# First norm's squares taken from the transposed input on chip, and the residual stream loaded later

## The chip, the cores and the metric

The kernel runs on one NeuronCore of a Trainium2 chip. Its engines run side by side, each through its own list of instructions in order: TensorE (PE: matmuls, with PEld for the loads of their stationary operand), VectorE (DVE), ScalarE (ACT), GpSimd (POOL) and SyncE (SP), which issues most of the DMAs. They wait for one another through semaphores. The metric is the device time of one execution in microseconds (us), the median of several runs; lower is better.

## The reference

One layer of a decoder in float32, on 256 tokens of width 1024: a gated feed-forward network (FFN) at half weight, a mixing layer with two branches, a second FFN at half weight, and a last norm. Cut to what matters here:

```python
def rmsnorm(x, g):
    y = xf * lax.rsqrt(jnp.mean(xf * xf, axis=-1, keepdims=True) + EPS)
    return y * g
def swiglu(x, w_gate, w_up, w_down):
    return (jax.nn.silu(x @ w_gate) * (x @ w_up)) @ w_down
h = x
h = h + 0.5 * swiglu(rmsnorm(h, ffn1_norm), ffn1_w_gate, ffn1_w_up, ffn1_w_down)
n = rmsnorm(h, mix_norm)
...
h = h + merged @ w_out
h = h + 0.5 * swiglu(rmsnorm(h, ffn2_norm), ffn2_w_gate, ffn2_w_up, ffn2_w_down)
return rmsnorm(h, final_norm)
```

The FFN's hidden width is 2816. The change concerns the first norm, `rmsnorm(h, ffn1_norm)` with h = x.

## The kernel before

**Precision and units.** The weights come from memory in units of 1 MB, each as two halves of 512 KB (`raw`, a ring of 7 buffers) on SP's queue. ACT casts each half to a high part and DVE subtracts to get a low part (`split`, L205 and L207); both go to `w`, a ring of 4 units. Each product is then three matmuls: high by high, high by low, low by high (`mm3`, L191 to L193). A unit's cast therefore waits until TensorE has left the unit four places earlier, and a load waits until DVE has left the half seven places earlier.

**The first FFN.** Its 11 chunks of 256 gate and 256 up columns take two units each: chunk c uses units 2c and 2c + 1, so chunk zero has units 0 and 1, chunk one units 2 and 3. TensorE runs 48 matmuls a chunk, 24 a unit. Unit 22 is the first of the down projection.

**The front.** The input and chunk zero's weights come together, transposed, in eight rows (`front`, 128 partitions; row k holds 256 columns of x for 128 features, then 512 of weights). ACT and DVE split each row as it lands (the loop over k), and TensorE follows with chunk zero (L491 to L495). x is only multiplied by the norm's gain there; the norm's factor per token, which is one over the root of the mean square, is applied to the chunk's result, in `glu` (L403, L405). Ahead of it TensorE runs 16 warm-up matmuls on zeros (L94).

**The norm's factor.** `square` (L231) squares the residual stream on ACT in four pieces of 128x512, `token_sums` (L237) adds the eight feature blocks on DVE in three steps, `sum_parts` splits the sum in a high and low part (`sqp`, ACT and DVE), and `token_factors` adds over partitions with one matmul by ones (`sums`, L247), takes each token's value by four reductions on DVE (L255) and raises it to the power -0.5 on POOL (L259).

**What is squared.** `h` is a second copy of x, loaded by two DMAs of 512 KB from the same array in memory (L480). It is also the residual stream to which the down projection adds its result (L318).

**The order.** TensorE and SP run in the order in which the code is written. ACT and DVE run in the written order too inside `in_order()` blocks; elsewhere a scheduler orders them. A call of `unit` makes splits up to a number of units ahead (`ALONE` 3, `PAIRED` 2), and those splits stand on ACT and DVE where the call stands. Before the change, `unit(f1, PAIRED)`, `unit(f1 + 1, PAIRED)` and `chunk(f1, nT, "f1", 1, [0])` put the splits of units 2 to 5 ahead of the squares. The matmul of the sums stands on TensorE behind chunk one.

**The hidden values' way.** After each chunk DVE transposes the gated product in 32x32 blocks (`f1t`), SP sends it to memory (`leave`, `f1way`), and brings it back in another order (`arrive`, `f1back`, one buffer) in six groups; `settle` splits a group to `f1h`, which the down projection uses. `move(c)` and `rest()` place these steps between the chunks and in the down projection. SP's queue carries them in order among the loads of the weights.

Of the kernel before, what the change touches and what calls it, by code (L numbers as in the profile page):

```python
# [20 lines left out]
S = 256  # L21
NT = S // P
DFF = 2816
KB = D // P
# [9 lines left out]
CH = 256  # L34
NC = DFF // CH
FIRST = 2
# [2 lines left out]

ALONE = RING - 1  # L40
PAIRED = RING - 2
WARM = 16


@with_exitstack
def block_kernel(ctx, tc, t, out):
    nc = tc.nc
# [10 lines left out]
    def bank(name):  # L58
        return psum.tile([P, 512], F32, tag="ps", name=name)
# [3 lines left out]
    h = act.tile([P, KB, S], F32, tag="h", name="h")  # L63
# [3 lines left out]
    ROW = S + 2 * CH  # L67
    front = act.tile([P, 2 * FB * S], F32, tag="aT", name="front")

    def load_front(queue, k, end, c0=0, c1=ROW):  # L70

        a, b = KB * (k + c0 > 0) + k * ROW + c0, KB + (end - 1) * ROW + c1
        queue.dma_start(front[:, a:b], t["first"][:, a:b])
# [18 lines left out]
    wps = bank("warm")  # L92
    for i in range(WARM):
        nc.tensor.matmul(wps[:, :S], zeros[:, :P], zeros, start=True, stop=True)  # L94
# [5 lines left out]
    def add_units(name, n):  # L100
        first = len(units)
        units.extend((name, i) for i in range(n))
        return first
# [3 lines left out]
    f1 = add_units("f1", 2 * NC)  # L107
# [16 lines left out]
    def unit_tile(i):  # L124
        a, b = t[units[i][0]].shape[2:]
        parts[i] = wp.tile([P, a, 2, b], F32R, tag="w", name=f"w{i}")

    def half(i, hf):
        a = t[units[i][0]].shape[2]
        return slice(hf * a // 2, (hf + 1) * a // 2)  # L130

    def fetch_to(n):

        while fetched[0] < min(n, 2 * len(units)):
            i, hf = divmod(fetched[0], 2)
            fetched[0] += 1
            name, u = units[i]
            _, p, a, b = t[name].shape
            raws[i, hf] = rawp.tile([P, a // 2, b], F32, tag="raw", name=f"raw{i}_{hf}")
            nc.sync.dma_start(raws[i, hf], t[name][u][:, half(i, hf), :])  # L140

    def split_half(later=False):

        i, hf = divmod(done_to[0], 2)
        if hf == 0:
            unit_tile(i)
        fetch_to(done_to[0] + RAW)
        done_to[0] += 1
        w, sl = parts[i], half(i, hf)
        return split(w[:, sl, 0, :], w[:, sl, 1, :], raws.pop((i, hf)), later)  # L150

    def split_to(n):
        while done_to[0] < 2 * min(n, len(units)):
            split_half()
        fetch_to(done_to[0] + RAW)

    def unit(i, ahead=PAIRED):
        split_to(i + 1 + ahead)
        return parts[i]
# [29 lines left out]
    def mm3(ps, st, mv_, first, last):  # L189
        (sh, sl), (mh, ml) = st, mv_  # L190
        nc.tensor.matmul(ps, sh, mh, start=first, stop=False)  # L191
        nc.tensor.matmul(ps, sh, ml, start=False, stop=False)  # L192
        nc.tensor.matmul(ps, sl, mh, start=False, stop=last)  # L193
# [10 lines left out]
    def split(hi, lo, src, later=False):  # L204
        nc.scalar.copy(hi, src)  # L205
        def rest():
            nc.vector.tensor_sub(lo, src, hi.bitcast(F32))  # L207
        return rest if later else rest()

    def alloc_T(name, tags):  # L210

        return [act.tile([P, 4, 2, S], F32R, tag=tag, name=f"{name}{c}") for c, tag in enumerate(tags)]
# [4 lines left out]
    def block_of(nT, k):  # L217
        return both_of(nT, k)[:, 0, :], both_of(nT, k)[:, 1, :]

    def in_order():  # L220

        return tc.manual_schedule(engines={mybir.EngineType.DVE, mybir.EngineType.Activation})
# [3 lines left out]
    def square(hh, pair, name, tag=None):  # L226

        if pair == 0:
            squares[name] = act.tile([P, KB, S], F32, tag=tag, name=f"sq{name}")
        two = slice(2 * pair, 2 * pair + 2)  # L230
        nc.scalar.activation(squares[name][:, two, :], hh[:, two, :], AF.Square, scale=D ** -0.5)  # L231

    def token_sums(name, engine=nc.vector):

        sq = squares[name]
        for n in (4, 2, 1):
            engine.tensor_add(sq[:, :n, :], sq[:, :n, :], sq[:, n:2 * n, :])  # L237

    def sum_parts(name):
        sq = squares[name]  # L240
        squares[name] = tmp.tile([P, 2, S], F32R, tag="hg", name=f"sqp{name}")
        split(squares[name][:, 0, :], squares[name][:, 1, :], sq[:, 0, :])
# [132 lines left out]
    def chunk(i0, nT, name, c, us=range(2), ps=None):  # L375


        if ps is None:
            ps = [bank(f"{name}_{c}{j}") for j in range(NT)]
        for u in us:  # L380
            w = unit(i0 + 2 * c + u, ALONE)
            for k in range(4):
                for j in range(NT):
                    st = tuple(p[:, j * P:(j + 1) * P] for p in block_of(nT, 4 * u + k))
                    mm3(ps[j], st, (w[:, k, 0, :], w[:, k, 1, :]), u + k == 0, u == 1 and k == 3)
        return ps
# [59 lines left out]


    nT = alloc_T("n1", ("nA", "nB"))
    for i in range(FIRST):
        unit_tile(i)  # L450
    for k in range(KB):
        if k > 1:
            load_front(nc.sync, k, k + 1)
        row = front[:, KB + k * ROW:KB + (k + 1) * ROW]
        x, w, g = row[:, :S], row[:, S:], front[:, k:k + 1]
        x_hi, x_lo = block_of(nT, k)
        hi, lo = (parts[k // 4][:, k % 4, q, :] for q in range(2))

        def x_high():
            nc.scalar.activation(x_hi, x, AF.Identity, scale=g)  # L460

        def x_low():
            nc.vector.scalar_tensor_tensor(x_lo, x, g, x_hi.bitcast(F32), op0=ALU.mult, op1=ALU.subtract)

        if k:
            x_high()
            x_low()
            split(hi, lo, w)
            continue

        with in_order():
            x_high()
            nc.vector.tensor_copy(hi[:, :CH], w[:, :CH])
            nc.scalar.copy(hi[:, CH:], w[:, CH:])
            x_low()
            for c in (slice(0, CH), slice(CH, 2 * CH)):
                nc.vector.tensor_sub(lo[:, c], w[:, c], hi[:, c].bitcast(F32))
    fetch_to(2 * FIRST + 4)
    for c in range(2):
        nc.sync.dma_start(h[:, 4 * c:4 * c + 4, :],  # L480
                          t["first"][:, KB:].rearrange("p (k c) -> p k c", k=KB)[:, 4 * c:4 * c + 4, :S])
    hidden = Hidden("f1")

    sums = [[bank(f"f1_0{j}") for j in range(NT)]]
    unit(f1, PAIRED)
    for k in range(KB):
        hi, lo = (parts[k // 4][:, k % 4, q, :] for q in range(2))
        st = [tuple(p[:, j * P:(j + 1) * P] for p in block_of(nT, k)) for j in range(NT)]
# [4 lines left out]
            nc.tensor.matmul(sums[0][j], st[j][1], hi, start=False, stop=False)  # L493
        for j in range(NT):
            nc.tensor.matmul(sums[0][j], st[j][0], lo, start=False, stop=k == KB - 1)  # L495
    unit(f1 + 1, PAIRED)

    with in_order():
        sums.append(chunk(f1, nT, "f1", 1, [0]))
        for pair in range(KB // 2):  # L500
            square(h, pair, "1", "nC")
        token_sums("1")
        sum_parts("1")
        chunk(f1, nT, "f1", 1, [1], sums[1])
        rs = token_factors("1")
        sums.append(chunk(f1, nT, "f1", 2))
        for c in range(2):
            hidden.glu(c, sums[c], rs)
    for c in range(2, NC):
        if c > 2:  # L510
            sums.append(chunk(f1, nT, "f1", c))
            for moved in (1, 2, 3) if c == 3 else (c,):
                hidden.move(moved)
        hidden.glu(c, sums[c], rs)
# [94 lines left out]
    for j in range(NT):  # L609
# [4 lines left out]
        for a0 in range(0, HEADS // 2, per):  # L614

            pair = [bank(f"sc{j}{a0}{two}") for two in range(2)]
# [104 lines left out]
    for f in range(KB):  # L721
        i = mb + 2 * (f // 4)
        ps = bank(f"pb{f}")
        c = slice(f % 4 * P, (f % 4 + 1) * P)
        for q, bT in enumerate((aoT, gmT)):
            w = unit(i + q)
# [12 lines left out]
    with in_order():  # L739
        down_features(mo, 4, lambda k: both_of(mT, k), 1.0, gain3, nT3, "3", "aT")  # L740
        hidden = Hidden("f2")
        sums = [chunk(f2, nT3, "f2", 0)]
# [139 lines left out]
```

## Time and profile before

| | |
|---|---|
| median of 3 runs | 536.08 us (535.26 to 536.53) |
| the profiled execution | 536.36 us |
| its span, first to last instruction | 534.6 us |
| mean granted clock of TensorE in it | 0.992 |
| TensorE (PE) busy | 522.3 us, 98% of the span |
| DVE busy | 367.6 us, 69% |
| ACT busy | 273.4 us, 51% |
| moved by DMA | 118.72 MB, 222 GB/s in the mean |

Times inside the execution are in us from the span's start. A row of the timeline has start, duration, engine, line, operation, output and input, and in brackets how long the engine stood idle before it and who released it; `x3` is three such instructions merged. A row with SPq is the issue of DMAs. A matmul of 512 columns is listed with 0.39 us, but they overlap: one starts every 0.23 us, so it is the distance of the starts that counts. A row of the waits has the waiting engine, tile and line, who was waited for, the us in total, the times and the longest. A row of the windows has the stretch and its length, then the busy time of PE, PEld, DVE, ACT and POOL with the count of instructions, then TensorE's granted clock (1.00 is full), the DMA engines' share and GB/s.

### The profile page before, as it was taken

The page shows a single profiled execution, that of the slowest core. Times are in us where ns is not written, and L with a number is a line of the kernel's source. Part 1 is how long each engine was busy: PE and PEld are TensorE (multiplying, and loading weights), DVE is VectorE, ACT ScalarE, POOL GpSimd, SP SyncE. Part 2 cuts the span into 40 slices and gives each one's busy share as a digit, 9 for nine tenths or more (in the row PEclk, how much of TensorE's full clock was granted, in tenths as well). Part 3 has the DMA queues.
Part 4 walks back from the last instruction along what each step waited for, and adds up shares of the span by engine and source line. Part 5 has one row for each costly group of instructions (what it writes and reads, how often), then busy time and mean ns, then how long its engine had stood idle before and what let it go on. Part 6 is the DMA issues. An engine that isn't in the chain of part 4 may idle for free.

```text
span 534.6 us, 7273 instructions
## 1 busy us (share of the span) xinstructions
PE 522.3 (98%) x2667; PEld 443.9 (83%) x2667; DVE 367.6 (69%) x568; ACT 273.4 (51%) x401; POOL 11.5 (2%) x20
## 2 busy tenths in 40 slices
PE   8969999999999999999999999999999999999995
PEld 6858888888888888888888999888888888888884
DVE  6676666575346498987999878689665665565424
ACT  7546355454335257546887645366453544463402
POOL 0010000000000001000000000001000000000002
PEclk9979999999999999999999999999999999999999
DMA  8976699869968507875469646339789779677302
GB/s 320 395 282 206 191 309 263 245 221 260 261 177 285 188 29 244 318 226 169 118 178 360 220 140 200 126 118 346 231 255 308 226 269 323 191 237 227 142 1 78
DMA packets 52420, 118.72 MB, mean 222 GB/s; under 512 B 6817, under 2 KB 26785, under 8 KB 52385
## 3 DMA queue, kind: packets, MB, share of 16 engines
q1 hardware_dynamic: 52096, 117.94, 68.0%
q8 instruction: 21, 0.34, 0.3%
q10 hardware_dynamic: 288, 0.33, 0.2%
q14 instruction: 15, 0.11, 0.1%
HBM read 108.81 MB, written 9.44 MB: 221 GB/s over the span
## 4 chain that ended last, share of the span: by engine, by line
PE 92%; DMA 4%; DVE 1%; ACT 1%; issue 0%; POOLq 0%; SPq 0%; DVEq 0%; POOL 0%; ACTq 0%
PE f L191 14%; PE f L192 14%; PE f L193 14%; PE acc L165 10%; PE pgate L165 6%; PE acc L170 5%; PE acch L191 4%; PE acch L192 4%; PE acch L193 4%; DMA raw<-in_f 3%; PE pgate L170 3%; PE pq L165 3%; PE pb L191 1%; PE pb L193 1%; PE pb L192 1%; PE pq L170 1%
## 5 line engine op out<-in xcount | busy, mean ns | idle before, releaser
L207 DVE TENSOR_TENSOR w<-raw,w 128x1024 fp32r<-128x1024 f32 x180 | 212.9, 1217 | 68.4 <-ACT w L205 67.8
L205 ACT CAST w<-raw 128x1024 fp32r<-128x1024 f32 x180 | 180.4, 1049 | 94.2 <-PE f L193 47.0
L191 PE MATMUL f<-w,n 128*128 128x512 f32 x336 | 131.7, 392 | 0.0
L192 PE MATMUL f<-w,n 128*128 128x512 f32 x336 | 131.5, 391 | 0.0
L193 PE MATMUL f<-w,n 128*128 128x512 f32 x336 | 131.4, 391 | 0.0
L193 PEld LDWEIGHTS f<-w,n 128*128 128x128 f32 x336 | 63.6, 189 | 13.4
L192 PEld LDWEIGHTS f<-w,n 128*128 128x128 f32 x336 | 63.6, 189 | 13.3
L191 PEld LDWEIGHTS f<-w,n 128*128 128x128 f32 x336 | 63.6, 189 | 13.2
L165 PE MATMUL acc<-f1h,w 128*128 128x512 f32 x176 | 43.4, 391 | 0.0
L165 PEld LDWEIGHTS acc<-f1h,w 128*128 128x128 f32 x176 | 31.9, 188 | 5.8
L191 PE MATMUL acch<-w,f2h 128*128 128x512 f32 x84 | 32.7, 389 | 0.0
L192 PE MATMUL acch<-w,f2h 128*128 128x512 f32 x84 | 32.7, 389 | 0.0
L193 PE MATMUL acch<-w,f2h 128*128 128x512 f32 x84 | 32.7, 389 | 0.0
L165 PE MATMUL pgate<-n,w 128*128 128x512 f32 x128 | 32.6, 394 | 0.0
L165 PEld LDWEIGHTS pgate<-n,w 128*128 128x128 f32 x128 | 23.0, 189 | 4.4 <-issue 0.2
L403 ACT ACTIVATE f2s<-f,rstd 128x256 f32<-128x256 f32 x22 | 10.3, 474 | 29.3 <-PE f L193 29.3
L170 PEld LDWEIGHTS acc<-f1h,w 128*128 128x128 f32 x176 | 23.5, 191 | 1.5
L405 DVE SCALAR_TENSOR_TENSOR f2a<-f,rstd,f2s 128x256 f32<-128x256 f32 x22 | 10.5, 476 | 20.7 <-ACT f2s L403 20.7
L170 PE MATMUL acc<-f1h,w 128*128 128x256 f32 x176 | 23.9, 282 | 0.0
L403 ACT ACTIVATE f1s<-f,rstd 128x256 f32<-128x256 f32 x22 | 10.2, 473 | 22.7 <-PE f L193 18.4
L318 DVE SCALAR_TENSOR_TENSOR h<-acc,h 128x256 f32<-128x256 f32 x32 | 13.6, 424 | 10.1 <-PE acc L165 8.1
L191 PEld LDWEIGHTS acch<-w,f2h 128*128 128x128 f32 x84 | 15.8, 188 | 3.3
(166 smaller groups left out, 635.9 us busy)
## 6 DMA issues: line engine op xcount, KB each, us to landing
raw<-in_f SPq DMA_DIRECT2D x84, 512.0 KB, 6.1
raw<-in_f1d SPq DMA_DIRECT2D x22, 512.0 KB, 5.9
raw<-in_f2d SPq DMA_DIRECT2D x22, 512.0 KB, 6.8
raw<-in_gate SPq DMA_DIRECT2D x16, 512.0 KB, 4.3
raw<-in_qk SPq DMA_DIRECT2D x8, 512.0 KB, 5.6
raw<-in_out SPq DMA_DIRECT2D x8, 512.0 KB, 4.6
f1way<-f1t SPq DMA_DIRECT2D x11, 256.0 KB, 6.3
f2way<-f2t SPq DMA_DIRECT2D x11, 256.0 KB, 6.0
```

The lines of the kernel that those rows point to most:

```text
L165: nc.tensor.matmul(ps, st, both.rearrange("p two n -> p (two n)"), start=first, stop=last)
L170: nc.tensor.matmul(ps[:, n:], st, both[:, 0, :], start=False, stop=False)
L191: nc.tensor.matmul(ps, sh, mh, start=first, stop=False)
L192: nc.tensor.matmul(ps, sh, ml, start=False, stop=False)
L193: nc.tensor.matmul(ps, sl, mh, start=False, stop=last)
L205: nc.scalar.copy(hi, src)
L207: nc.vector.tensor_sub(lo, src, hi.bitcast(F32))
L318: nc.vector.scalar_tensor_tensor(h[:, c, :], acc[c][:, q * S:(q + 1) * S], scale, h[:, c, :], op0=ALU.mult, op1=ALU.add)
L403: nc.scalar.activation(sg, ps[j][:, :CH], AF.Silu, scale=rs[j])
L405: nc.vector.scalar_tensor_tensor(a, ps[j][:, CH:], rs[j], sg, op0=ALU.mult, op1=ALU.mult)
```

## The change

Three things are edited. The squares read x in `front`, that is the copy that is already on the chip for the matmuls, and not `h`. They stand behind the splits of unit 2 (`split_to(f1 + 3)`; `f1` is 0), with the halves of unit 3 split one before and one after the additions; all of this is inside `in_order()`. `h` is loaded later, by the same two DMAs, behind chunk two's code and the first products. Beside that, `WARM` is 17 for 16, the loop over k splits its rows inside `in_order()` for every k, two more halves are fetched in one go, and the tile of the hidden values is allocated later, since it takes the memory of `front`.

```diff
-WARM = 16
+WARM = 17
...
     nT = alloc_T("n1", ("nA", "nB"))
+
+    def inputs_of(rows):
+        return rows.rearrange("p (k c) -> p k c", k=KB)[:, :, :S]
...
-        if k:
-            x_high()
-            x_low()
-            split(hi, lo, w)
-            continue
-
         with in_order():
             x_high()
-            nc.vector.tensor_copy(hi[:, :CH], w[:, :CH])
-            nc.scalar.copy(hi[:, CH:], w[:, CH:])
+            if k == 0:
+
+                nc.vector.tensor_copy(hi[:, :CH], w[:, :CH])
+                nc.scalar.copy(hi[:, CH:], w[:, CH:])
+            else:
+                nc.scalar.copy(hi, w)
             x_low()
-            for c in (slice(0, CH), slice(CH, 2 * CH)):
+            for c in (slice(0, CH), slice(CH, 2 * CH)) if k == 0 else (slice(0, 2 * CH),):
                 nc.vector.tensor_sub(lo[:, c], w[:, c], hi[:, c].bitcast(F32))
-    fetch_to(2 * FIRST + 4)
-    for c in range(2):
-        nc.sync.dma_start(h[:, 4 * c:4 * c + 4, :],
-                          t["first"][:, KB:].rearrange("p (k c) -> p k c", k=KB)[:, 4 * c:4 * c + 4, :S])
-    hidden = Hidden("f1")
+    fetch_to(2 * FIRST + 6)
 
     sums = [[bank(f"f1_0{j}") for j in range(NT)]]
-    unit(f1, PAIRED)
...
-    unit(f1 + 1, PAIRED)
 
     with in_order():
-        sums.append(chunk(f1, nT, "f1", 1, [0]))
+        x = inputs_of(front[:, KB:KB + KB * ROW])
+        split_to(f1 + 3)
         for pair in range(KB // 2):
-            square(h, pair, "1", "nC")
+            square(x, pair, "1", "nC")
+        split_half()
         token_sums("1")
+        split_half()
         sum_parts("1")
-        chunk(f1, nT, "f1", 1, [1], sums[1])
+        sums.append(chunk(f1, nT, "f1", 1))
         rs = token_factors("1")
         sums.append(chunk(f1, nT, "f1", 2))
+        hidden = Hidden("f1")
         for c in range(2):
             hidden.glu(c, sums[c], rs)
+    for c in range(2):
+        nc.sync.dma_start(h[:, 4 * c:4 * c + 4, :], inputs_of(t["first"][:, KB:])[:, 4 * c:4 * c + 4])
```

On ACT, at chunk one, the rows before the change are these; `w2` is unit 2, `raw2_0` its first half, `sq1` the squares and `sqp1` their split sum:

```order
L205 CAST w2_177<-raw2_0_164 128x2x512
L205 CAST w2_177<-raw2_1_166 128x2x512
L205 CAST w3_242<-raw3_0_168 128x2x512
L205 CAST w3_242<-raw3_1_170 128x2x512
L205 CAST w4_255<-raw4_0_178 128x2x512
L205 CAST w4_255<-raw4_1_180 128x2x512
L205 CAST w5_262<-raw5_0_182 128x2x512
L205 CAST w5_262<-raw5_1_186 128x2x512
L231 ACTIVATE sq1_297<-h_80 128x512 x4
L205 CAST sqp1_305<-sq1_297 128x256
```

and in the changed kernel, on ACT at the same place:

```order
L205 CAST w2_252<-raw2_0_186 128x2x512
L205 CAST w2_252<-raw2_1_188 128x2x512
L231 ACTIVATE sq1_263<-front_81 128x512 x4
L205 CAST w3_268<-raw3_0_190 128x2x512
L205 CAST w3_268<-raw3_1_192 128x2x512
L205 CAST sqp1_278<-sq1_263 128x256
L205 CAST w4_283<-raw4_0_194 128x2x512
```

The squares have moved ahead of unit 3, the cast of their sum ahead of unit 4, and they read `front`. On DVE, at the same place, the changed kernel has (before, the three additions and `sqp1` stood behind `w5`):

```order
L207 TENSOR_TENSOR w2_252<-raw2_1_188,w2_252 128x2x512
L207 TENSOR_TENSOR w3_268<-raw3_0_190,w3_268 128x2x512
L237 TENSOR_TENSOR sq1_263<-sq1_263 128x1024
L237 TENSOR_TENSOR sq1_263<-sq1_263 128x512
L237 TENSOR_TENSOR sq1_263<-sq1_263 128x256
L207 TENSOR_TENSOR w3_268<-raw3_1_192,w3_268 128x2x512
L207 TENSOR_TENSOR sqp1_278<-sq1_263,sqp1_278 128x256
L207 TENSOR_TENSOR w4_283<-raw4_0_194,w4_283 128x2x512
```

The additions now stand between the halves of unit 3. On SP the two loads of `h` have moved from ahead of `raw4_0` to between `raw12_0` and `raw12_1`. TensorE's rows are the same but for one more warm-up matmul.

The scheduler also puts some later rows of ACT and DVE in another order. On ACT, where the first FFN's chunks end, the rows before are (`f1s100` and `f1s101` belong to the last chunk's gated product, `f1back3` and `f1back4` to the fourth and fifth group of hidden values):

```order
L205 CAST w24_1086<-raw24_1_970 128x1024
L205 CAST f1h_174<-f1back3_1035 128x8x4x32
L403 ACTIVATE f1s100_1123<-f1_100_1051,rstd1_354 128x256
L403 ACTIVATE f1s101_1128<-f1_101_1052,rstd1_354 128x256
L205 CAST w25_1197<-raw25_0_974 128x1024
L205 CAST w25_1197<-raw25_1_1003 128x1024
L205 CAST f1h_174<-f1back4_1192 128x8x4x32
```

and in the changed kernel, on ACT at the same place:

```order
L205 CAST w24_1108<-raw24_1_992 128x1024
L403 ACTIVATE f1s100_1145<-f1_100_1073,rstd1_373 128x256
L403 ACTIVATE f1s101_1150<-f1_101_1074,rstd1_373 128x256
L205 CAST w25_1219<-raw25_0_996 128x1024
L205 CAST w25_1219<-raw25_1_1025 128x1024
L205 CAST f1h_443<-f1back3_1057 128x8x4x32
L205 CAST f1h_443<-f1back4_1214 128x8x4x32
```

The fourth group's cast has moved from ahead of the last products to behind unit 25; DVE's subtraction moves likewise.

## The prediction

> **What bounds the kernel now.** I read the page first, then who waits for whom on TensorE, and then the timeline around the one long wait.
>
> ```profile
> span 534.6 us, 7273 instructions
> PEclk9979999999999999999999999999999999999999
> PE 92%; DMA 4%; DVE 1%; ACT 1%; issue 0%; POOLq 0%; SPq 0%; DVEq 0%; POOL 0%; ACTq 0%
> PE sums L247 <- DVE sqp L207: 4.5, 1, 4.5
> PE warm L94 <- DVE zeros L91: 1.2, 1, 1.2
> ```
>
> The chain that ended last lies 92% on TensorE, and the list of waits has for its matmuls, over the whole span, only the two quoted and one of 0.4 at the start (its row stands further down). So TensorE is the bound nearly everywhere, and what keeps it still is worth its full length. The one wait of size is the single matmul at L247, which adds the first norm's squares. It costs more than the 4.5 us of its row, as the third slice of the clock row (7 tenths) hints. The next fence is TensorE's timeline: start, duration, instruction.
>
> ```profile
> 17.45 0.39 PE L193 MATMUL f<-w,n 128*128 128x512 f32 x1
> 27.65 0.39 PE L193 MATMUL f<-w,n 128*128 128x512 f32 x1
> 32.58 0.79 PE L247 MATMUL sums<-sqp,ones 128*128 128x512 f32 x1 [4.54 <-DVE sqp L207]
> 33.17 0.63 PE L191 MATMUL f<-w,n 128*128 128x512 f32 x1
> 37.44 0.49 PE L192 MATMUL f<-w,n 128*128 128x512 f32 x1
> 38.00 0.40 PE L191 MATMUL f<-w,n 128*128 128x512 f32 x1
> ```
>
> From chunk one's third matmul (17.45; so its first was at 17.00) to its last (27.65) lie 45 steps: (27.65 - 17.45) / 45 = 0.227 us each. The sums matmul could have started at 27.65 + 0.23 = 27.88; it started at 32.58, **4.70 late**. Then the pace is wrong: from 33.17 to 37.44 there are 10 steps of 0.427. The windows say why (TensorE's granted clock is the third value from the right):
>
> ```profile
> 30.00:31.00 1.00, 0.00 (x0) 0.00 (x0) 0.97 (x2) 0.00 (x0) 0.00 (x0) 0.91 1.06 422
> 37.00:38.00 1.00, 1.00 (x5) 0.81 (x3) 1.00 (x2) 0.00 (x0) 1.00 (x1) 0.68 0.66 217
> ```
>
> The clock fell to half inside the stall (0.91 over that microsecond, so about 0.18 of it at half: near 30.82) and came back near 37.64 (0.68, so 0.64 of it at half). The sums matmul and the 12 after it took 38.00 - 32.58 = 5.42 us; 13 steps at 0.227 are 2.95. So **2.47 us** more are lost after the stall.
>
> Why was the sum late? ACT's and DVE's timelines:
>
> ```profile
> 14.15 1.05 ACT L205 CAST w<-raw 128x1024 fp32r<-128x1024 f32 x1 [0.23 <-DMA raw<-in_f]
> 16.73 1.06 ACT L205 CAST w<-raw 128x1024 fp32r<-128x1024 f32 x1 [0.25 <-DMA raw<-in_f]
> 23.66 3.44 ACT L205 CAST w<-raw 128x1024 fp32r<-128x1024 f32 x3 [1.52 <-DMA raw<-in_f]
> 27.01 2.18 ACT L231 ACTIVATE sq<-h 128x512 f32<-128x512 f32 x4
> 31.66 0.40 ACT L205 CAST sqp<-sq 128x256 fp32r<-128x256 f32 x1 [2.48 <-DVE sq L237]
> 40.98 2.00 ACT L205 CAST w<-raw 128x1024 fp32r<-128x1024 f32 x2 [5.13 <-issue]
> 22.17 1.23 DVE L207 TENSOR_TENSOR w<-raw,w 128x1024 fp32r<-128x1024 f32 x1 [3.12 <-ACT w L205]
> 29.22 2.41 DVE L237 TENSOR_TENSOR sq<-sq 128x1024 f32<-128x1024 f32 x3 [0.86 <-ACT sq L231]
> 32.10 0.42 DVE L207 TENSOR_TENSOR sqp<-sq,sqp 128x256 fp32r<-128x256 f32 x1 [0.47 <-ACT sqp L205]
> ```
>
> In the program the squares stand behind the casts of units 2 to 5. The casts just ahead of them end at 23.66 + 3.44 = 27.10; squares (2.18), three additions (2.41), cast and subtraction then end at 32.5. TensorE is at this matmul 4.7 us earlier.
>
> **The change part by part.** I lay the new order of ACT and DVE out with the durations above, keeping unit 2's and unit 3's arrivals.
>
> *Squares and sums behind unit 2's splits.* ACT ends unit 2's second cast at 15.20; the squares (2.18) take it to 17.4. Unit 3's two casts (2.00 a pair; its second half was cast at 16.73, so both are there) run to 19.4. DVE: the first half of unit 3 subtracts from 18.4 to 19.7, the additions to 22.1, the second half to 23.3. ACT casts the sum at 22.1 to 22.5; DVE subtracts from 23.3 to **23.7**. TensorE wants it at 27.88, so it is 4.2 early and the wait goes: **-4.70**. No half-clock stretch follows: **-2.47**.
>
> *What is late next.* Unit 3's first half is needed by TensorE at 17.00 + 24 x 0.227 = 22.4 and its second 12 steps on, at 25.2; they are ready at 19.7 and 23.3, so 2.7 and 1.9 early. Unit 4 is needed at 28.1: ACT casts it from 22.5 to 24.5, DVE ends the halves at 24.9 and 26.2. Units 5 and 6 follow, DVE done with them near 31.0, for 33.6 and 39.0. Cost: 0. The squares now read the transposed input's strided rows; no row shows that form. Bounds: nothing, or as slow as a 128x1024 cast (1.05 each against 2.18 / 4 = 0.55), 2.0 us in all, which spends unit 3's 1.9 and stalls TensorE by 0.1. I take nothing, the nearest row being the same square on the same shape.
>
> *The factors.* The four reductions keep their place behind unit 6's splits.
>
> ```profile
> 35.32 0.28 DVE L255 CUSTOM_DVE_ANT_0 own<-sums,ident 128x128 bf16<-128x128 f32 x1
> 36.83 1.62 POOL L259 TENSOR_TENSOR rstd<-ms,nhalf 128x2 f32<-128x2 f32 x1 [35.10 <-DVE ms L255]
> 44.34 0.48 DVE L405 SCALAR_TENSOR_TENSOR f1a<-f,rstd,f1s 128x256 f32<-128x256 f32 x1
> ```
>
> The reductions and POOL's start lie 36.83 - 35.32 = 1.5 apart; with DVE free at 31.0 that and POOL's 1.62 end at 34.1. The first gated product stands behind unit 8's casts, which wait until TensorE has left unit 4 (40.98 now, 33.6 then, done at 35.6). So the factors are in time, and the PSUM banks come free as far ahead of chunk three as before (product at 44.34 to 44.82, chunk three at 38.00 + 36 x 0.227 = 46.2; both move with TensorE). Cost: 0.
>
> *The load of h.* Two DMAs of 512 KB leave the place ahead of unit 4's weights and return between the halves of unit 12.
>
> ```profile
> 39.00:46.00 7.00, 7.00 (x33) 5.79 (x32) 3.88 (x7) 3.50 (x6) 0.00 (x0) 1.00 0.69 227
> DMA to landing us min/median/max: 9.6/9.8/10.1
> L318 DVE SCALAR_TENSOR_TENSOR h<-acc,h x32: 423/424/425, 184.9 to 349.0; 128x256 f32<-128x256 f32 x32
> ```
>
> The engines moved 227 GB/s there, with a share of 0.69, so there is room; even if this landing took the 9.8 us of now, h is first used at 184.9. On SP two issues stand ahead of unit 12's second half, which TensorE needs only in chunk six, at 28.1 + 4 x 10.9 = 71.7. Cost between 0 and, if the queue had no room, 1 MB at 227 GB/s (4.6 us) spent out of over 20 us of lead: 0.
>
> *One more warm-up matmul.* It fills the gap ahead of the first real one.
>
> ```profile
> 5.15 1.22 PE L491 MATMUL f<-w,n 128*128 128x256 f32 x4 [0.37 <-ACT n L460]
> 6.17 0.97 PE L493 MATMUL f<-w,n 128*128 128x512 f32 x2
> 6.99 0.63 PE L495 MATMUL f<-w,n 128*128 128x512 f32 x2
> ```
>
> The gap is 0.37 and a warm-up step at half clock about 0.21, so it fits. If not, it costs 0.21; if it brought the full clock ahead of the pair at 6.17 (0.41 a step against 0.23), it gains 0.37. I take 0, keeping both ends.
>
> *The scheduler's other moves.* DVE and ACT carry the same instructions later on, some exchanged. The one that matters is the settling of the fourth hidden group (f1h from f1back3), which falls behind the casts of unit 25 and stands next to the fifth's. The rows are ACT, DVE, SP's issues and, last, TensorE's chain at units 26 and 28:
>
> ```profile
> 144.48 1.05 ACT L205 CAST f1h<-f1back 128x1024 fp32r<-128x1024 f32 x1 [8.70 <-DMA f1back<-f1way]
> 157.86 0.62 ACT L205 CAST f1h<-f1back 128x512 fp32r<-128x512 f32 x1 [8.53 <-DMA f1back<-f1way]
> 135.16 2.32 DVE L207 TENSOR_TENSOR w<-raw,w 128x1024 fp32r<-128x1024 f32 x2
> 146.70 4.62 DVE L207 TENSOR_TENSOR w<-raw,w 128x1024 fp32r<-128x1024 f32 x4
> 159.47 3.50 DVE L207 TENSOR_TENSOR w<-raw,w 128x1024 fp32r<-128x1024 f32 x3 [0.27 <-ACT w L205]
> 135.74 2.97 SPq L425 DMA_DIRECT2D f1back<-f1way  x4
> 149.59 1.80 SPq L425 DMA_DIRECT2D f1back<-f1way  x4
> 155.66 3.65 PE acc L165 x16
> 166.79 3.65 PE acc L165 x16
> ```
>
> On the old time scale: DVE ends unit 25 at 135.16 + 2.32 = 137.5 and the fourth group's split of the same size (1.23) at 138.7. The fifth group's way back reuses that buffer, so SP issues it at 138.7 and not at 135.74: **3.0 later**. All behind it in order, on SP the weights of units 28 to 30, on ACT the casts of units 26 and 27, moves by 3.0. Unit 26 is then ready at 146.70 + 2.3 + 3.0 = 152.0 for 155.66. The sixth group's way back moves from 149.59 to 152.6; behind its split come unit 28's two (before: two of the three from 159.47, so to 161.8; then: to 164.8), for TensorE at 166.79. The margin falls from 5.0 to 2.0 and still covers it: 0.
>
> *Sum.* 536.36 (the profiled execution, 1.76 around its span) - 4.70 - 2.47 = **529.2**, a span of 527.4. That execution is 0.28 over the median of the runs (536.08; 535.26 to 536.53).
>
> [...]
>
> **The rivals.** *The wait moves into chunk one*: squares and additions stand ahead of unit 3's and unit 4's splits, and TensorE waits there. The margins speak against it (1.9 and 2.7). If the work there took 4 us longer, the stall would be 2.1: 531.3.
> *The wait moves to the down projection*: the sixth group's trip took 8.3 us from issue to cast (149.59 to 157.86) and the fifth's 8.7 (135.74 to 144.48); one that takes 2.0 longer than the sixth's reaches TensorE. For it speaks that two trips now stand in a tighter chain; against it, that none of these waits reaches TensorE now. At a trip of 10.3 to 12.3 us it costs 0 to 2.0: up to 531.2.
> *Slower*: the same place, with a trip so long that TensorE halts past 4.7 us and the clock falls as it did here. Stall and slow stretch together must pass 7.2, which takes a trip 2.0 + 4.7 = 6.7 longer, 15.0 us; at 17 us it gives 529.2 + 6.7 + 2.5 = 538.4.
> [...]
> *It does not do what it says*: the sum is early in the program, but TensorE still waits about as long, for instance if unit 3's weights landed 9 us late and held DVE. Their casts at 16.73 speak against it: 536.
>
> **How the numbers follow.** The full gain (529.2): 0.80. A wait in chunk one: 0.05. A wait in the down projection: 0.09. Slower: 0.03. Nothing gained: 0.03. About 0.2% (1.1 us) is what a measurement of this kernel can tell from no change; so faster 0.94, same 0.03, slower 0.03. The range runs from 529.2 less the 0.28 to the median, 0.8 of spread between runs and the warm-up's 0.37, which is 527.7, to the small waits' 531.3.
>
> **What would show it.** In the changed kernel's waits the row of L247 is gone or under a microsecond; the granted clock is 1.00 in every microsecond from 20 to 40; chunk two's first matmul starts near 28.1; the squares start near 15.2 and sqp is done near 23.7; h's landing has nobody waiting; the sixth f1h split is followed by unit 28's with TensorE never idle near 160. It is wrong if TensorE shows a new wait of over 1 us, at unit 3 or 4 or in the down projection, or if the later part of the span, from chunk three to the end, is longer than now.

## The result, and the profile after

| | before | changed |
|---|---|---|
| median | 535.71 us (535.26 to 536.53, 4 runs) | 528.66 us (528.44 to 529.01, 4 runs) |
| ratio | | 0.9867 (0.985 to 0.9884) |
| profiled execution | 536.36 | 528.46 |
| its span | 534.6 | 526.8 |

The changed kernel is 7.05 us, or 1.3%, faster. Of all runs told of here, one of the kernel with 16 warm-up matmuls was disturbed (1062 us) and is left out.

The changed kernel's page: span, TensorE's granted clock in 40 slices, the chain that ended last by engine, and below them the one row that its list of waits has for TensorE's matmuls.

```profile
span 526.8 us, 7279 instructions
PEclk9999999999999999999999999999999999999998
PE 98%; DVE 0%; issue 0%; POOLq 0%; ACT 0%; DVEq 0%; POOL 0%; ACTq 0%
PE warm L94 <- DVE zeros L91: 1.2, 1, 1.2
```

The 7 in the clock's third slice is gone, the DMA's part has left the chain, and the wait at L247 is no longer listed. The rows of the place itself, TensorE first, then ACT, then DVE:

```profile
16.36 0.39 PE L191 MATMUL f<-w,n 128*128 128x512 f32 x1
27.01 0.40 PE L193 MATMUL f<-w,n 128*128 128x512 f32 x1
27.25 0.40 PE L247 MATMUL sums<-sqp,ones 128*128 128x512 f32 x1
15.17 2.18 ACT L231 ACTIVATE sq<-front 128x512 f32<-128x512 f32 x4
17.26 1.99 ACT L205 CAST w<-raw 128x1024 fp32r<-128x1024 f32 x2
21.90 0.41 ACT L205 CAST sqp<-sq 128x256 fp32r<-128x256 f32 x1 [2.65 <-DVE sq L237]
18.32 1.23 DVE L207 TENSOR_TENSOR w<-raw,w 128x1024 fp32r<-128x1024 f32 x1 [1.80 <-ACT w L205]
21.78 1.22 DVE L207 TENSOR_TENSOR w<-raw,w 128x1024 fp32r<-128x1024 f32 x1
22.92 0.41 DVE L207 TENSOR_TENSOR sqp<-sq,sqp 128x256 fp32r<-128x256 f32 x1
```

The squares start at 15.17 and the split sum is ready at 22.92 + 0.41 = 23.33. TensorE asks for it at 27.25, one step after chunk one's last matmul, with no idle time in between.

The 7.8 us of the two spans fall in three pieces. The sums matmul cuts each execution in two: what lies behind it was 534.6 - 32.58 = 502.02 and is now 526.8 - 27.25 = 499.55, so **2.47** less. From chunk one's first matmul to the sums it was 32.58 - 17.00 = 15.58 and is 10.89, so **4.69** less. Chunk one itself starts at 16.36 instead of 17.00, **0.64** earlier. The same cut is made for the experiments (us; the last column is the span less the sums' start):

| profiled execution | chunk one starts | sums start | behind them |
|---|---|---|---|
| before | 17.00 | 32.58 | 502.0 |
| changed | 16.36 | 27.25 | 499.6 |
| source alone, 16 warm-ups | 18.45 | 29.33 | 499.5 |
| source alone, 17 warm-ups | 16.59 | 29.87 | 501.2 |
| place alone | 16.82 | 29.23 | 499.5 |
| changed, squares behind unit 6 | 16.96 | 32.02 | 502.4 |
| before, wait filled | 16.54 | 32.85 | 499.7 |
| changed, h early | 16.75 | 27.63 | 499.6 |

### The profile page after: what moved, and what is told of

The parts are those of the page before. It is cut to its first block, busy times and chain, and to the rows that moved or that the text cites. A ratio compares the mean times of both kernels' runs of the same rounds, so it can differ in the third digit from the quotient of the medians.

```text
span 526.8 us, 7279 instructions
## 1 busy us (share of the span) xinstructions
PE 519.4 (99%) x2668; PEld 441.6 (84%) x2668; DVE 367.0 (70%) x568; ACT 273.0 (52%) x401; POOL 11.5 (2%) x20
## 4 chain that ended last, share of the span: by engine, by line
PE 98%; DVE 0%; issue 0%; POOLq 0%; ACT 0%; DVEq 0%; POOL 0%; ACTq 0%
PE f L192 14%; PE f L193 14%; PE f L191 14%; PE acc L165 10%; PE pgate L165 6%; PE acc L170 5%; PE acch L193 4%; PE acch L192 4%; PE acch L191 4%; PE pgate L170 3%; PE pq L165 3%; PE pb L193 1%; PE pb L191 1%; PE pb L192 1%; PE pq L170 1%; PE pu L165 1%
```

## The experiments

My theory: every microsecond by which the sums matmul is late is paid in full, and an idle time like the 4.54 us of before costs the half clock (2.47 there) on top. The rivals: the half speed after the wait has another cause; it is the place on ACT and DVE, or the source of the squares, or the place of h's load, or the warm-up, that does all.

### The wait filled with work

```diff
+        for i in range(40):
+            nc.tensor.matmul(wps[:, :S], zeros[:, :P], zeros, start=True, stop=True)
         rs = token_factors("1")
```

> The kernel before with 40 matmuls on zeros (256 columns, results unused) between chunk one and the sums matmul, so that TensorE is busy in the wait but the wait stays. Theory (of the gain 4.70 us are the wait and about 2.5 the half clock behind it): the clock stays at 1.00 from 28 to 38, the sums matmul still starts near 32.6, and the time is 535.7 - 2.5 = 533.2. Rival (the slow steps after the wait are not from idling, but from the data arriving): 535.7. Rival (the filling matmuls overrun the wait): over 535.7.

Measured: 534.05 us (533.75 to 534.44), ratio 0.9968 (0.9955 to 0.9981) to its own runs of before at 535.76 (533.93 to 536.85). The sums matmul in the profile, and the windows around it (third value from the right: the granted clock):

```profile
32.85 0.50 PE L247 MATMUL sums<-sqp,ones 128*128 128x512 f32 x1 [0.89 <-DVE sqp L207]
32.00:33.00 1.00, 0.15 (x1) 0.15 (x2) 0.42 (x1) 1.00 (x2) 0.00 (x0) 1.00 0.82 328
33.00:34.00 1.00, 1.00 (x5) 0.83 (x6) 0.68 (x1) 1.00 (x2) 0.00 (x0) 1.00 0.11 41
```

The sum is as late as ever, but the clock stays at 1.00, and what lies behind takes 499.7 instead of 502.0. So the slow steps came from TensorE's idling. The medians differ by 1.7 and not 2.5, because not every execution of before loses the whole stretch. The mean granted clock that is on record for each run shows it: of the 14 runs of before beside this one, two at 0.997 took 533.9 and 534.1, as long as the filled ones (0.997 to 0.999); five at 0.994 or 0.995 took 535.4 to 535.7; seven at 0.991 or 0.992 took 535.8 to 536.9.

### The source alone

The squares read `front`, h is loaded later, the squares keep their place behind unit 5.

```diff
-    for c in range(2):
-        nc.sync.dma_start(h[:, 4 * c:4 * c + 4, :], ...
...
+        x = front[:, KB:KB + KB * ROW].rearrange("p (k c) -> p k c", k=KB)[:, :, :S]
         for pair in range(KB // 2):
-            square(h, pair, "1", "nC")
+            square(x, pair, "1", "nC")
```

> The kernel before with one part of the change alone: the squares read the transposed input that is on chip, and h is loaded later, but the squares keep their old place behind the splits of units 2 to 5. Theory (every microsecond by which the sums matmul is late is paid in full, and the half clock comes on top only when TensorE idles long): without h the eighth half of the weights lands about 2.6 us earlier (two loads of 512 KB at 1.3), so the casts end near 24.5 instead of 27.1 and the sums matmul starts near 30.0, still about 2.1 us late; no half clock after it. Span near 534.6 - 2.6 - 2.5 = 529.5, time 531.3. Rival (the place on ACT and DVE is all, the source nothing): 535.7 as before. Rival (the clock falls even after 2 us of idling): 533.7.

Measured: 530.80 us (529.61 to 532.91), ratio 0.9909 (0.9889 to 0.9929). The time is near what I wrote, but the profile shows another way to it. ACT's squares, DVE's last step of the sum, then TensorE's sums matmul, the start of chunk one and two pairs of chunk zero:

```profile
22.73 2.19 ACT L231 ACTIVATE sq<-front 128x512 f32<-128x512 f32 x4
27.83 0.43 DVE L207 TENSOR_TENSOR sqp<-sq,sqp 128x256 fp32r<-128x256 f32 x1 [0.47 <-ACT sqp L205]
29.33 0.40 PE L247 MATMUL sums<-sqp,ones 128*128 128x512 f32 x1
18.45 0.39 PE L191 MATMUL f<-w,n 128*128 128x512 f32 x1
7.15 1.05 PE L491 MATMUL f<-w,n 128*128 128x512 f32 x2
9.71 0.72 PE L491 MATMUL f<-w,n 128*128 128x512 f32 x2
```

The squares came earlier than expected (22.73 for 24.5), and the sum was ready at 27.83 + 0.43 = 28.26. Chunk zero ran at half pace until about 9.9 (pairs at 0.43 a step; in the trace of before, where the pair at 6.17 took 0.41 a step, the windows from 6 to 7 list a granted clock of 1.00), so chunk one began at 18.45, TensorE asked for the sum only at 29.33, and it was no longer late. This is one execution: another of the six took 532.91 at a mean granted clock of 0.994, against 0.997 to 0.999 for the rest, which points to the second rival there.

By the traces, what made the squares earlier at the old place is not that they read `front`: before the change they did not wait for h either (no idle time ahead of them at 27.01). It is that h's two loads no longer stand ahead of unit 4's weights. ACT's cast of unit 4's first half, before and then here (merged with the second half):

```profile
21.08 1.05 ACT L205 CAST w<-raw 128x1024 fp32r<-128x1024 f32 x1 [3.29 <-DMA raw<-in_f]
```

```profile
18.01 2.25 ACT L205 CAST w<-raw 128x1024 fp32r<-128x1024 f32 x2 [0.30 <-DMA raw<-in_f]
```

The new source is what lets the load move. No run reads `front` at the old place with h loaded early, so the two are not taken apart by a run.

I took the late start for a matter of the warm-up matmuls (this kernel has 16), and ran it with 17:

> The run with the source alone (530.8, 529.6 to 532.9), but with 17 warm-up matmuls. There the squares' sum was ready near 28.3, about 0.9 later than TensorE wants it after a quick start. Theory (what made that kernel 2.1 slower than the changed one was mostly its slow start, with the place of the squares costing 0.9): sums at 28.3 plus the 499.5 from there to the end plus 1.8 around the span, 529.6, with all runs within 1 us. Rival (the place of the squares cost the 2.1): 530.8.

Measured: 531.83 us (530.80 to 532.87), ratio 0.9923 (0.9908 to 0.9938), three runs near 530.9 and three near 532.8. My expectation fell and the rival's price was nearer. ACT's last cast ahead of the squares, the sums matmul, and two windows:

```profile
23.34 1.05 ACT L205 CAST w<-raw 128x1024 fp32r<-128x1024 f32 x1 [1.68 <-DMA raw<-in_f]
29.87 0.50 PE L247 MATMUL sums<-sqp,ones 128*128 128x512 f32 x1 [2.25 <-DVE sqp L207]
31.00:32.00 1.00, 1.00 (x5) 0.76 (x4) 1.00 (x2) 1.00 (x2) 0.00 (x0) 0.59 0.04 16
34.00:35.00 1.00, 1.00 (x4) 0.76 (x4) 1.00 (x3) 0.00 (x0) 0.88 (x1) 0.70 0.73 266
```

Behind unit 5 the squares hang on its last half, whose load is issued at 15.19, when DVE has left the buffer. Here its cast ended at 23.34 + 1.05 = 24.39, with 16 warm-ups at 22.83, although the load was issued at 15.15 there; why it landed later is not shown. So the wait is 2.25, and half clock from about 31.2 to 34.6 costs 501.2 - 499.5 = 1.7 more. Three of the six runs are about 1.9 above the other three. Only one of them (532.87) has a profile, but the mean granted clocks fit: 0.994 to 0.996 for the three longer ones, 0.997 and 0.998 for the others. Taking the squares from the chip and loading h later, without moving the squares, is worth some 4 to 5 us, and not the same in each run.

### The place alone

The changed kernel, but the squares read `h`, which is loaded at the old place.

```diff
-    fetch_to(2 * FIRST + 6)
+    fetch_to(2 * FIRST + 4)
+    for c in range(2):
+        nc.sync.dma_start(h[:, 4 * c:4 * c + 4, :], ...
...
-            square(x, pair, "1", "nC")
+            square(h, pair, "1", "nC")
```

> The changed kernel with the other part alone: the squares stand at the new place behind unit 2's splits, but read h, which is loaded at the old place, ahead of unit 4's weights. Theory: h lands near 18.4 and 19.4 (issued at 8.6 and 9.6, 9.8 to landing), so the squares end near 20.5 instead of 17.4, unit 3's two low parts near 22.7 and 26.3 for 22.4 and 25.2, and the sums are ready at 26.7 for 27.9: TensorE waits about 1 us at unit 3 and not at the sums; 529.8 (1.1 over the changed kernel). Rival (the squares held up by h delay everything behind them as they did, so that the place brings nothing without the source): 535.7.

Measured: 530.44 us (530.36 to 530.87), ratio 0.9902 (0.9884 to 0.992). ACT's squares, then the row of TensorE's waits:

```profile
18.25 1.15 ACT L231 ACTIVATE sq<-h 128x512 f32<-128x512 f32 x2 [3.05 <-DMA h<-in_first]
19.73 1.15 ACT L231 ACTIVATE sq<-h 128x512 f32<-128x512 f32 x2 [0.32 <-DMA h<-in_first]
PE f L192 <- DVE w L207: 0.9, 2, 0.5
```

The squares start at 18.25 and 19.73, near the 18.4 and 19.4 forecast for h, and the wait that is left stands at unit 3 and no longer at the sums: chunk one took 29.23 - 16.82 = 12.4 instead of 10.9. So the place brings 5.3 us even with the late source. The two parts overlap, since the sum has only to be there when TensorE asks for it: each alone brings 4 to 5.3, both 7.05. With the place in, the source brings the last 1.8; with the source in, the place brings 3.0 (531.83 against 528.78 for the changed kernel run beside it).

### The squares behind unit 6

The changed kernel, with the squares and additions behind unit 6's splits. That is one unit later than before the change, when they stood behind unit 5's.

```diff
-        split_to(f1 + 3)
+        split_to(f1 + 7)
...
-        split_half()
         token_sums("1")
-        split_half()
         sum_parts("1")
```

> The changed kernel with the squares and additions in one piece behind unit 6's splits instead of unit 2's; all else as in the changed kernel. Theory: ACT ends unit 6's casts near 25.2 (two more than the 22.7 at which it ended unit 5's in the run with the source alone), squares, additions, cast and subtraction take 5.5 more, so the sums matmul starts near 30.8 for 27.4: 3.4 late, paid in full, and at this length the clock falls in some executions (0 to 2.5 more): 532.1 to 534.5. Rival (only the data's path from memory mattered, and the place among the splits does not): 528.7.

Measured: 535.60 us (534.88 to 536.86), ratio 0.9992 (0.998 to 1.0004): nothing is left of the gain, with the new source, the late load and 17 warm-ups all in. (At the old place itself, behind unit 5, these three kept about 4 us of it: the source alone with 17 warm-ups.) ACT's casts of unit 6 and the squares, the sums, and the clock:

```profile
24.29 1.05 ACT L205 CAST w<-raw 128x1024 fp32r<-128x1024 f32 x1 [1.50 <-DMA raw<-in_f]
25.49 1.06 ACT L205 CAST w<-raw 128x1024 fp32r<-128x1024 f32 x1 [0.15 <-DMA raw<-in_f]
26.44 2.19 ACT L231 ACTIVATE sq<-front 128x512 f32<-128x512 f32 x4
32.02 0.80 PE L247 MATMUL sums<-sqp,ones 128*128 128x512 f32 x1 [4.02 <-DVE sqp L207]
36.00:37.00 1.00, 1.00 (x4) 0.77 (x3) 0.67 (x1) 0.00 (x0) 0.10 (x1) 0.50 0.25 57
```

I had the casts end at 25.2; they waited for the weights and ended at 26.5, so the sums were late by 4.2 instead of 3.4. With the half clock (502.4 against 499.6) that is 7.0 in the profiles; the medians lie 6.9 apart, and this one 1.1 above my range. With the same source, then, the place decides: the sum is ready at 23.33 behind unit 2, at 28.26 or 29.81 behind unit 5, and near 32.0 behind unit 6.

### The place of h's load, and the warm-up

The changed kernel with h loaded ahead of unit 4's weights again:

> The changed kernel with h loaded at its old place, ahead of unit 4's weights; the squares still read the input on chip. Theory (the load's place costs nothing, since unit 4's casts stand behind the sum's cast at 22 and its weights are there by then): 528.7, the same as the changed kernel. Rival (the load's place is worth the 2.6 us that its 1 MB takes): 531.3.

Measured: 528.60 us (528.45 to 528.86), ratio 0.9865 (0.9848 to 0.9883). The load's place is worth nothing here; sums at 27.63, TensorE idle nowhere behind it.

Before with 17 warm-up matmuls, the changed kernel with 20, and with 16 twice (beside the changed kernel itself once more):

> The kernel before with 17 warm-up matmuls. Theory (a late start is hidden there, since TensorE waits at the sums for ACT and DVE whatever it does before; what moves the time there is the half clock behind the wait): 535.7, no change. Rival (the extra warm-up is worth its 0.5 to 1 us in any kernel): 534.9.

> The changed kernel with 20 warm-up matmuls. Three more steps of 0.21 or 0.11 end between 5.1 and 5.6, while the first real matmul could start at 5.0 to 5.4. Theory (the gap is nearly closed already; more only delays chunk zero): 528.7 to 529.2. Rival (a better filled start brings the clock up earlier): 528.2.

> The changed kernel with 16 warm-up matmuls instead of 17. In the profile of the run with the source alone (16 warm-ups) chunk one started at 18.45 instead of 16.36, since the clock was at half until about 9.9. [...]

> The changed kernel with 16 warm-up matmuls, again, since its first runs were few (528.5, 528.6, 530.4). Theory (the 17th keeps a bad clock window away): most runs near 528.6, but some at 530 or more, none of which the changed kernel shows. Rival (no effect): no run above 529.1.

> The changed kernel once more, beside the next two. Both theories: 528.4 to 529.1 as before.

Measured: before with 17, 536.36 us, ratio 1.0004 (0.9995 to 1.0013), no change. The changed kernel with 20, 528.86 (528.77 to 529.50); with 17 once more, 528.78 (528.61 to 529.29); with 16, 528.5, 528.6 and 530.4 at first and 528.57 to 528.93 in four runs later. For 16 I had put the median over 529.3, on an estimate that no run bears out; it fell. Six of these seven runs are as fast as with 17, so no effect of the 17th on the usual run is shown. Whether it keeps a run like that at 530.4 away stays open: it is a single run (its mean granted clock was 0.996, for 0.998 in the two beside it), and eight runs with 17 had none.

## Why the prediction held, step by step

**The wait, -4.70.** Right: 4.69. The sum was ready at 23.33 for 23.7 forecast, and in time as the trace of before let one work out from the durations alone.

**The half clock, -2.47.** Right: 2.47 in the profile, and the run with the wait filled shows that it is a cost of idling. In the medians it is less (1.7 by the filled run), since the mean granted clock of the executions of before differs (0.991 to 0.997). That the gain in the medians, 7.05, still lies so near the forecast 4.70 + 2.47 = 7.17 is in part luck: an earlier start, which the sum does not have (0.6 in the profiles), makes up for it.

**What is late next.** Unit 3's halves were ready at 19.55 and 23.00 for 19.7 and 23.3, and TensorE did not wait. With the squares read from h the same margins ran out, at the same place, for 1.5 us against 1.1 expected.

**The factors, 0.** Right: POOL was done with them at 31.61 + 1.62 = 33.2, for 34.1 forecast, and TensorE waits for nothing behind the sums.

**The squares on strided rows, 0.** Right: 2.18 for the four, as from h.

**The load of h, 0.** Right: it lands in 7.7 to 8.7 us, with nobody waiting, and early or late makes no difference.

**The extra warm-up, 0, with -0.37 as an end.** Within its bounds nothing is shown for it. What the sum lacked is the start: 0.64 of the 0.7 us between 529.2 and the profiled 528.46, from the first row of the input and the pace of the first matmuls. ACT's first row, before and then changed:

```profile
4.59 0.51 ACT L460 ACTIVATE n<-front 128x256 fp32r<-128x256 f32 x1 [1.85 <-DMA front<-in_first]
```

```profile
4.42 0.51 ACT L464 ACTIVATE n<-front 128x256 fp32r<-128x256 f32 x1 [1.68 <-DMA front<-in_first]
5.69 0.63 PE L490 MATMUL f<-w,n 128*128 128x512 f32 x2
6.17 0.74 PE L492 MATMUL f<-w,n 128*128 128x512 f32 x2
```

The input landed 0.17 earlier, and the pair at 5.69 runs at 0.24 a step where before the pair at 6.17 took 0.41. But before with 17 warm-ups began chunk one at 16.97, and the changed kernel with 16 at 16.38 and 16.49, so it is not the warm-up. The prediction puts nothing on the other edit at the start, the rows split in order in the loop over k, and no run has it alone: the eight profiles with it begin chunk one between 16.36 and 16.96, the five without it between 16.54 and 18.45. These overlap, so how much of the 0.64 is the edit and how much chance stays open. It also became visible only now: before, the sums waited for ACT and DVE, and their start did not follow TensorE's (chunk one at 17.00 and, with the wait filled, 16.54; the sums at 32.58 and 32.85).

**The settling that the scheduler moved, 0.** Right, with more to spare than forecast. ACT, DVE, SP's issue and TensorE's chain in the changed kernel:

```profile
136.71 1.05 ACT L205 CAST f1h<-f1back 128x1024 fp32r<-128x1024 f32 x1 [7.81 <-DMA f1back<-f1way]
151.23 6.90 DVE L207 TENSOR_TENSOR w<-raw,w 128x1024 fp32r<-128x1024 f32 x6 [0.26 <-ACT w L205]
130.64 1.80 SPq L425 DMA_DIRECT2D f1back<-f1way  x4
158.97 3.65 PE acc L165 x16
```

The fifth group's way back was issued at 130.64, which is 138.4 on the old scale (7.8 later), near the forecast 138.7. But the trip took 136.71 - 130.64 = 6.1 us instead of 8.7, so the delay was given back: unit 28 was ready at 151.23 + 2 x 1.15 = 153.5 for 158.97, a margin of 5.4 and not 2.0. Of these 2.6, 1.2 lie in the issuing (the four issues took 1.80 instead of 2.97); why the trip was shorter was not tried.

**The rivals.** None of them took place in the changed kernel. A wait in chunk one is real when the squares come later (the place alone). The prediction priced the two smaller rivals at the stall alone, up to 531.3 and 531.2; no run shows that a stall of up to 2.1 us costs only itself. The source alone with 17 warm-ups speaks against that price: after 2.25 us of waiting the clock fell to half for 3.4 us (near 31.2 to 34.6), so such a rival could have cost 1.7 us more than its stall. A shorter wait, the 0.89 us that was left in the filled run, left the clock at 1.00 up to 39.

## What to carry to other kernels

A wait of the bounding engine is worth its length and what its clock does after it (here 4.69 and 2.47 us): count the steps behind the wait until their pace is back. Work that an engine will ask for at a known moment belongs on its makers' queues as far ahead as its inputs allow, and no transfer needs to be waited for when the same data is already on chip in another form; but check what it pushes back there, by the due time of each piece. Once the wait is gone, what it hid (here the start, 0.64 us) sets the end.

## What the runs showed of the hardware that was not expected

A gap of 2.25 us in TensorE's work was enough for the half clock in one execution, and it came 1.3 us after work had begun again (sums at 29.87, clock down near 31.2). The loss comes in steps: over the 46 runs of before whose mean granted clock is on record, 3 lie at 0.997 (533.9 to 534.1 us), 12 at 0.994 or 0.995 (534.9 to 535.7) and 31 at 0.991 or 0.992 (535.6 to 536.9). A step of 0.003 of 534 us is 1.6 us of clock lost, that is, by this estimate, about 3.2 us at half. The profiled execution, at 0.992, has 6.8 us of it in one piece (30.82 to 37.64), the source alone with 17 warm-ups, at 0.995, has 3.4, and the filled run, at 0.998, none from 20 to 39. The chance of each execution shows in chunk zero too: over the profiles here chunk one began between 16.36 and 18.45, latest where the first matmuls ran longest at half pace (0.43 a step until about 9.9, the source alone with 16 warm-ups).
